# Attention tiles of a decoder step driven by one task, a group of three tiles' parts pinned on TensorE

## The chip, the core and the metric

The kernel runs on one core of a Trainium2 chip. The time is that of the device for one execution, in microseconds (us). Of the core's engines TensorE (PE) multiplies matrices, VectorE (DVE), ScalarE (ACT) and GpSimd (POOL) do elementwise work, reductions and copies, and SyncE (SP) issues most of the transfers.

## What is computed

One step of a two-layer decoder over 1024 prompt tokens and 64 sample tokens (8 sequences of 8), width 1024. Layer 0 mixes by retention (6 heads of 128), layer 1 by dilated sliding-window attention (three groups of four heads of 64), and both also by attention of four heads into 256 memory tokens. Each layer ends with an output projection, a layer norm and a gated feed-forward part. The change touches the two attentions over prompt tokens:

```python
def memory_attention(q, mem_kv):
    sc = jnp.einsum('bshd,bnhd->bhsn', q, mem_kv[:, :, 0]) * MEM_HEAD_DIM ** -0.5
    p = jax.nn.softmax(sc, axis=-1)
    return jnp.einsum('bhsn,bnhd->bshd', p, mem_kv[:, :, 1])

def dilated_prompt(q, k, v, window, dil):
    ...
    sc = jnp.where(valid[:, None], einsum(qb, kk) * d ** -0.5, -jnp.inf)   # this block's keys and the previous block's
    lse = jax.nn.logsumexp(sc, axis=-1)
    p = jnp.exp(sc - lse[..., None])
    o = jnp.einsum('brchqk,brckhd->brcqhd', p, vv)
```

The groups have window and dilation (128, 1), (512, 4) and (2048, 16); their outputs are merged by their softmax denominators.

## The kernel before

All is in fp32. A projection (`dense`) is emulated by three products of split operands (lines L316 to L318, `pd` is the bank they add into). Tokens lie in nine tiles of 128 (eight of prompt, one half tile of samples) and three chunks of 512, 256 and 320 columns.

An attention tile covers 128 tokens and two heads of 64. It has three parts on TensorE, with other engines between them. First the scores, one matmul for each head, which use 64 rows of the array (`S`, L462 in memory attention, L1279 in layer B); the two heads' operands lie in partitions 0 to 63 and 64 to 127. VectorE takes the maximum and ScalarE the exponential (for memory attention VectorE also divides by the sum: L466 to L472; for layer B L1282 to L1287). Then TensorE transposes the probabilities (`mpt` L477, `bpt` L1292) and VectorE copies them (L479, L1294). Last come the output matmuls, which fill 64 columns of the array (`mo` L485, `bo` L1300), and ScalarE copies the result (L149). The trace counts one such fp32 matmul as two instructions, and a transpose as one.

What sets the order: attention tiles are generators which `yield` after each part. The scheduler `S` (class `Streams`) holds them in a queue. A dense step calls `S.tick()` now and then, which lets the first `window` of the queue's active tasks advance in turn; a yielded number is the number of ticks until the task may go on. So the order in which instructions are written mixes dense steps and the parts of several tiles. The tile framework then orders the instructions of each engine once more, by when it expects their operands to be ready, so that a task's instruction can move in front of or behind dense matmuls. Banks of PSUM are shared: four of the pool `pa` serve scores, transposes and outputs.

`mem_prompt(l, T, ...)` is one task for each token tile and covers two pairs of heads in turn (j = 0, 1); main adds eight of them for layer 0 and `layer_b` eight for layer 1. In layer B, `UNITS` lists six units (gi, j): group gi (0 is the local one with dilation 1), pair of heads j. `unit` adds eight `attend` tasks for gi = 1 and 2. For gi = 0 `local_chunk` drives the tiles of one chunk, two at a time, with a `yield` after each part. `row_scores` and `sample` are the samples' attention, `caches` writes cache rows, and `v_tiles` transposes values (`vtr`).

Of the kernel before, what the change touches and what calls it, by code (L numbers as in the profile page):

```python
# [87 lines left out]
def trunk(ctx: ExitStack, tc: tile.TileContext, A: dict, O: dict, g128, g8):  # L88
# [13 lines left out]
    mm = nc.tensor.matmul  # L102
# [10 lines left out]
    SR = (2, 1)  # L113
    SY = (2, 3)
# [254 lines left out]
    def mem_front(sts):  # L369
        mh = [slot([P, 4, 256], F32R, "mh") for _ in range(2)]  # L370
        ml = [slot([P, 4, 256], F32R, "ml") for _ in range(2)]
        for t in range(2):
            for half in range(2):
                b = bank("mtr")
                for i in range(4):
                    nc.tensor.transpose(b[:, i * P:(i + 1) * P], sts[t][:, (half * 4 + i) * P:(half * 4 + i + 1) * P], ident)
# [5 lines left out]
    def mem_kv(l, mh, ml, kt, dst):  # L382
# [3 lines left out]
        for u in range(4):  # L386
# [6 lines left out]
            for i in range(2):  # L393
                nc.tensor.transpose(acc[i][:, u * P:(u + 1) * P], t[:, i * P:(i + 1) * P], ident)
# [5 lines left out]
    def x_task():  # L400
# [10 lines left out]
        for T in range(9):  # L411
# [3 lines left out]
            for half in range(2):  # L415
                b = bank("xtr")
                for i in range(4):
                    nc.tensor.transpose(b[:, i * P:i * P + n], st[:n, (half * 4 + i) * P:(half * 4 + i + 1) * P], ident[:n, :n])
# [35 lines left out]
    def mem_prompt(l, T, kv, kt):  # L454
        yield from wait(("qm", l, chunk_of(T)))
        ts_ = slice(T * P, (T + 1) * P)
        for j in range(2):
            ssum = small(2, "mss")
            sb = [bank("S"), bank("S")]
            for h in range(2):  # L460
                hs = slice(h * 64, (h + 1) * 64)
                mm(sb[h][:, :256], lhsT=mx[hs, 6 + j, ts_], rhs=kt[hs, j, :], start=True, stop=True)  # L462
            nm = small(2, "mnm")
            Pt = rt([P, 2, 256], "mp")
            for h in range(2):
                nc.vector.tensor_reduce(out=nm[:, h:h + 1], in_=sb[h][:, :256], op=ALU.max, axis=AX.X, negate=True)  # L466
                nc.scalar.activation(Pt[:, h, :], sb[h][:, :256], AF.Exp, bias=nm[:, h:h + 1],
                                     accum_out=ssum[:, h:h + 1])
            rs = small(2, "mrs")
            nc.vector.reciprocal(rs, ssum)  # L470
            for h in range(2):
                nc.vector.tensor_scalar(Pt[:, h, :], Pt[:, h, :], rs[:, h:h + 1], None, op0=ALU.mult)  # L472
            yield 1
            pb = bank("mpt")
            for h in range(2):
                for t in range(2):
                    nc.tensor.transpose(pb[:, (2 * h + t) * P:(2 * h + t + 1) * P], Pt[:, h, t * P:(t + 1) * P], ident)  # L477
            pT = rt([P, 512], "mpT")
            nc.vector.tensor_copy(pT, pb)  # L479
            yield 1  # L480
            ob = bank("mo")
            for t in range(2):
                for h in range(2):
                    v0 = 256 + (2 * j + h) * 64
                    mm(ob[h * 64:(h + 1) * 64, :P], lhsT=kv[:, t, v0:v0 + 64], rhs=pT[:, (2 * h + t) * P:(2 * h + t + 1) * P],  # L485
                       start=(t == 0), stop=(t == 1))
            acopy(mx[:, 6 + j, ts_], ob[:, :P])
            yield 1
        done.add(("memT", l, T))

    def mem_sample(l):
# [24 lines left out]
        for b in range(0, 8, 2):  # L516
            kcs, nxt = nxt, [load(b + 2, 0), load(b + 3, 0)]
            kTs = []
            for kc in kcs:
                kb = bank("mkb")  # L520
                for j in range(2):
                    for t in range(2):
                        nc.tensor.transpose(kb[:, (2 * j + t) * P:(2 * j + t + 1) * P], kc[:, t, j * P:(j + 1) * P], ident)
# [21 lines left out]
        for f in range(2):  # L545
            for t in range(2):
                nc.tensor.transpose(pb[:, (2 * f + t) * P:(2 * f + t + 1) * P], Pt[:, f, t * P:(t + 1) * P], ident)
# [15 lines left out]
        for i in range(4):  # L563
            nc.tensor.transpose(tb[:, i * P:(i + 1) * P], on[:, i * P:(i + 1) * P], ident)
# [311 lines left out]
    def y_tiles(c, tiles, grow, brow):  # L876
# [3 lines left out]
        for half in range(2):  # L880
            yield from wait(("y", c, half))
            hs = slice(half * 512, half * 512 + 512)
            for T, n in tiles:
# [3 lines left out]
                for i in range(4):  # L887
                    nc.tensor.transpose(b[:n, i * P:(i + 1) * P], mx[:, half * 4 + i, T * P:T * P + n], ident)
# [87 lines left out]
    def retention(h, qT, kT, V, dmat, dq):  # L976
# [3 lines left out]
        for c in range(3):  # L980
# [14 lines left out]
            for i in range(ni):  # L995
                nc.tensor.transpose(kb[:, i * P:(i + 1) * P], kT[:, c0 + i * P:c0 + (i + 1) * P], ident)
            if samp:
                nc.tensor.transpose(kb[:64, 256:384], kT[:, NP:NT], ident)
# [78 lines left out]
            for i, r in rows:  # L1077
                nc.tensor.transpose(otb[:, i * P:i * P + r], on[:r, i * P:(i + 1) * P], ident[:r, :r])
# [85 lines left out]
    def layer_b():  # L1164
# [35 lines left out]
        def unit(gi, j):  # L1200
# [4 lines left out]
            if gi > 0:  # L1205
# [38 lines left out]
        def caches(gi, j, Kt, V):  # L1244
# [4 lines left out]
            nc.tensor.transpose(bk[:64, :P], Kt[:, NP:NT], ident)  # L1249
# [4 lines left out]
            for q in range(0, len(tiles), 4):  # L1254
                sub = tiles[q:q + 4]
                b = bank("kto")
                for i, T in enumerate(sub):
                    nc.tensor.transpose(b[:, i * P:(i + 1) * P], Kt[:, T * P:(T + 1) * P], ident)
# [6 lines left out]
        def attend(gi, j, T, Qt, Kt, V, oo, om):  # L1265
# [24 lines left out]
            for h in range(2):  # L1290
                for t in range(nt):
                    nc.tensor.transpose(pb[:, (h * nt + t) * P:(h * nt + t + 1) * P], Pt[:, h, t * P:(t + 1) * P], ident)  # L1292
# [24 lines left out]
        def local_chunk(j, c, Qt, Kt, V):  # L1317
# [358 lines left out]
```

## Time and profile before

| | us |
|---|---|
| median of 3 runs | 2707.31 (2706.66 to 2708.17) |
| the profiled execution | 2703.15 |
| its span in the trace | 2701.3 |
| TensorE busy | 2606.2 (96%) |
| VectorE busy | 1821.3 (67%) |
| ScalarE busy | 1200.6 (44%) |
| GpSimd busy | 933.4 (35%) |

A share is an average over all stages. TensorE's is over 90% in nearly all of the 40 slices of the span, and the mean granted clock of the whole run is 0.99 of full speed. Which instruction TensorE waited for, and where, is read from the table of waits; what an instruction costs in its place is read from the starts in the timeline.

### The profile page before, as it was taken

The page shows a single profiled execution, that of the slowest core. Times are in us where ns is not written, and L with a number is a line of the kernel's source. Part 1 is how long each engine was busy: PE and PEld are TensorE (multiplying, and loading weights), DVE is VectorE, ACT ScalarE, POOL GpSimd, SP SyncE. Part 2 cuts the span into 40 slices and gives each one's busy share as a digit, 9 for nine tenths or more (in the row PEclk, how much of TensorE's full clock was granted, in tenths as well). Part 3 has the DMA queues.
Part 4 walks back from the last instruction along what each step waited for, and adds up shares of the span by engine and source line. Part 5 has one row for each costly group of instructions (what it writes and reads, how often), then busy time and mean ns, then how long its engine had stood idle before and what let it go on. Part 6 is the DMA issues. An engine that isn't in the chain of part 4 may idle for free. (4 is left out here: it accounts for less than half of the span.)

```text
span 2701.3 us, 48271 instructions
## 1 busy us (share of the span) xinstructions
PE 2606.2 (96%) x18057; PEld 2360.9 (87%) x18057; DVE 1821.3 (67%) x3843; ACT 1200.6 (44%) x2617; POOL 933.4 (35%) x1118
## 2 busy tenths in 40 slices
PE   8999999999999999999999999989999999999997
PEld 8778888798999989999977777768989998899997
DVE  4534345578777798666684775777987768866666
ACT  4432223344544554444455555544454445344434
POOL 0012223654444443333530111136444444433335
PEclk9999999999999999999999999999999999999998
DMA  7131111134333333332322553552324433433332
GB/s 252 32 95 51 54 48 56 58 93 132 113 113 112 125 100 106 121 103 89 116 91 87 159 163 91 157 148 87 102 91 133 125 119 121 133 114 114 98 96 84
DMA packets 417818, 289.22 MB, mean 107 GB/s; under 512 B 21360, under 2 KB 403120, under 8 KB 415920
## 3 DMA queue, kind: packets, MB, share of 16 engines
q1 hardware_dynamic: 417584, 286.13, 34.4%
q8 instruction: 143, 2.34, 0.4%
q14 instruction: 91, 0.75, 0.1%
HBM read 272.25 MB, written 40.83 MB: 116 GB/s over the span
## 5 line engine op out<-in xcount | busy, mean ns | idle before, releaser
L152 POOL TENSOR_TENSOR wl<-rawu,wh 128x256 fp32r<-128x256 f32 (+1 forms) x560 | 449.7, 827 | 834.1 <-ACT wh L149 748.6
L149 ACT ACTIVATE wh<-raw 128x512 fp32r<-128x512 f32 (+1 forms) x628 | 388.8, 623 | 569.7 <-DVE raw L152 200.2
L316 PE MATMUL pd<-xh,wl 128*128 128x512 f32 (+2 forms) x1200 | 419.4, 350 | 0.8 <-DVE t L439 0.7
L152 DVE TENSOR_TENSOR wl<-raw,wh 128x512 fp32r<-128x512 f32 x460 | 341.8, 747 | 115.3 <-ACT wh L149 111.4
L317 PE MATMUL pd<-xl,wh 128*128 128x512 f32 (+2 forms) x1200 | 407.7, 340 | 0.2 <-DVE xl L152 0.2
L318 PE MATMUL pd<-xh,wh 128*128 128x512 f32 (+2 forms) x1200 | 406.9, 340 | 0.0
L764 PE MATMUL gb<-xh,wl 128*128 128x256 f32 (+1 forms) x1232 | 357.4, 290 | 7.1 <-DVE up L152 3.3
L766 PE MATMUL gb<-xh,wh 128*128 128x256 f32 (+1 forms) x1232 | 356.4, 289 | 0.0
L765 PE MATMUL gb<-xl,wh 128*128 128x256 f32 (+1 forms) x1232 | 353.8, 287 | 0.0
L152 POOL TENSOR_TENSOR wl<-raw,wh 128x256 fp32r<-128x256 f32 x336 | 270.5, 830 | 120.9 <-ACT wh L149 105.5
L764 PE MATMUL pd<-xh,wl 128*128 128x256 f32 (+1 forms) x880 | 255.3, 290 | 7.9 <-DVE up L152 3.9
L149 ACT ACTIVATE wh<-rawu 128x512 fp32r<-128x512 f32 (+1 forms) x280 | 170.9, 614 | 198.9 <-PE pd L816 70.5
L316 PEld LDWEIGHTS pd<-xh,wl 128*128 128x128 f32 x1200 | 227.3, 190 | 36.1 <-issue 16.3
L766 PE MATMUL pd<-xh,wh 128*128 128x256 f32 (+1 forms) x880 | 254.1, 289 | 0.0
L765 PE MATMUL pd<-xl,wh 128*128 128x256 f32 (+1 forms) x880 | 252.1, 286 | 0.0
L317 PEld LDWEIGHTS pd<-xl,wh 128*128 128x128 f32 x1200 | 227.8, 190 | 25.2 <-issue 7.5
L318 PEld LDWEIGHTS pd<-xh,wh 128*128 128x128 f32 x1200 | 227.3, 189 | 24.0 <-issue 5.1
L764 PEld LDWEIGHTS gb<-xh,wl 128*128 128x128 f32 x1232 | 232.7, 189 | 10.0 <-DVE wl L152 3.1
L765 PEld LDWEIGHTS gb<-xl,wh 128*128 128x128 f32 x1232 | 234.4, 190 | 0.6 <-DVE xl L152 0.2
L766 PEld LDWEIGHTS gb<-xh,wh 128*128 128x128 f32 x1232 | 232.4, 189 | 0.0
L814 PE MATMUL gb<-hid,wl 128*128 128x512 f32 (+2 forms) x528 | 174.0, 331 | 4.3 <-ACT hid L149 2.2
L764 PEld LDWEIGHTS pd<-xh,wl 128*128 128x128 f32 x880 | 165.6, 188 | 10.3 <-issue 4.6
(344 smaller groups left out, 6130.5 us busy)
## 6 DMA issues: line engine op xcount, KB each, us to landing
rawu<-in_w_ffn_in_dram SPq DMA_DIRECT2D x88, 512.0 KB
raw<-in_w_ffn_in_dram SPq DMA_DIRECT2D x88, 512.0 KB
raw<-in_w_out_dram SPq DMA_DIRECT2D x32, 512.0 KB
raw<-in_w_ffn_out_dram SPq DMA_DIRECT2D x32, 512.0 KB
rawu<-in_w_ffn_out_dram SPq DMA_DIRECT2D x32, 512.0 KB
out_wins_dram<-in_cache_win_kv_g_dram SPq DMA_DIRECT2D x64, 256.0 KB
qb<-scr_q SPq DMA_DIRECT2D x64, 256.0 KB
raw<-in_w_in_a_dram SPq DMA_DIRECT2D x26, 512.0 KB
```

The source lines that it names most:

```text
L149: nc.scalar.activation(out, in_, AF.Copy, scale=scale)
L152: (eng or nc.vector).tensor_tensor(out=out, in0=a, in1=b, op=op)
L316: mm(out, lhsT=wl, rhs=rh, start=(k == 0), stop=False)
L317: mm(out, lhsT=wh, rhs=rl, start=False, stop=False)
L318: mm(out, lhsT=wh, rhs=rh, start=False, stop=(k == kt - 1))
L764: mm(ps, lhsT=wl[:, k], rhs=XH[:, i, k], start=start and k == 0, stop=False, skip_group_check=True)
L765: mm(ps, lhsT=wh[:, k], rhs=XL[:, i, k], start=False, stop=False, skip_group_check=True)
L766: mm(ps, lhsT=wh[:, k], rhs=XH[:, i, k], start=False, stop=stop and k == 3, skip_group_check=True)
L814: mm(ps, lhsT=wl[:, k], rhs=hid[k][:, 0, ts_], start=first, stop=False)
```

## The change

Matmuls and transposes on TensorE are issued through wrappers that can pin an instruction: it then stays behind the instruction written before it on the same engine, by an edge that only keeps the order. Inside `together()` all of them are pinned, and the first one after it too. A new function `staggered` drives the tiles of one task. Each of its steps starts one more tile and advances all that are under way, the oldest first: the output matmuls of one tile, the transposes of the next and the scores of a third are written one behind the other, inside `together()`. Then it yields a gap: 2 ticks (`MG`, `AG`), and 1 in `local_chunk`. Memory attention becomes one task of 16 pieces (`mem_part`, tile and j), the eight `attend` tiles of a unit one task, and `local_chunk` uses `staggered` in place of two tiles at a time. Ticks, rates and all other constants stay.

```diff
@@ -99,7 +99,27 @@
     pa = pool("pa", 4, space=bass.MemoryType.PSUM)
 
 
-    mm = nc.tensor.matmul
+    pin = {"all": False, "next": False}
+
+    def pinned(ins):
+
+        if pin["all"] or pin["next"]:
+            tc.keep_in_program_order(ins)
+            pin["next"] = pin["all"]
+        return ins
+
+    def mm(*args, **kw):
+        return pinned(nc.tensor.matmul(*args, **kw))
+
+    def transpose(*args):
+        return pinned(nc.tensor.transpose(*args))
+
+    @contextmanager
+    def together():
+        pin["all"] = pin["next"] = True
+        yield
+        pin["all"] = False
+
     dma = nc.sync.dma_start
     S = Streams(3)
     LNY = ((1, 5, 2), (3, 11, 5), (4, 7, 2))
...
@@ -111,6 +131,7 @@
     PA = (6, 4)
     WIN_ = (5, 4)
     SR = (2, 1)
+    MG, AG = 2, 2
     SY = (2, 3)
     RY = (2, 2, 5)
     done = set()
@@ -330,7 +351,7 @@
         b = bank("vtr")
         for i, T in enumerate(tiles):
             a = src(T)
-            nc.tensor.transpose(b[:a.shape[1], i * P:(i + 1) * P], a, ident)
+            transpose(b[:a.shape[1], i * P:(i + 1) * P], a, ident)
         full = [T for T in tiles if T < 8]
         n = len(full)
         if n:
...
@@ -451,42 +472,61 @@
                 S.tick()
             done.add(("qm", l, c))
 
-    def mem_prompt(l, T, kv, kt):
-        yield from wait(("qm", l, chunk_of(T)))
+    def staggered(gens, gap):
+
+
+        live, gens = deque(), deque(gens)
+        while gens or live:
+            if gens:
+                g = gens.popleft()
+                if isinstance(g, tuple):
+                    yield from wait(g[0])
+                    g = g[1]
+                live.append(g)
+            with together():
+                for g in list(live):
+                    if next(g, None) is None:
+                        live.remove(g)
+            yield gap
+
+    def mem_prompt(l, kv, kt):
+
+        yield from staggered([(("qm", l, chunk_of(T)), mem_part(l, T, j, kv, kt)) for T in range(8) for j in range(2)], MG)
+
+    def mem_part(l, T, j, kv, kt):
...
+        yield 1
+        pb = bank("mpt")
...
+        yield 1
+        ob = bank("mo")
...
-            acopy(mx[:, 6 + j, ts_], ob[:, :P])
-            yield 1
-        done.add(("memT", l, T))
+        acopy(mx[:, 6 + j, ts_], ob[:, :P])
+        if j:
+            done.add(("memT", l, T))
...
@@ -1225,9 +1265,8 @@
                 ost = slot([P, 1056], F32, "ost")
                 oo = ost[:, 0:NP].rearrange("p (x r) -> p r x", r=dil)
                 om = ost[:, NP:1056].rearrange("p (t s) -> p t s", t=8)
-                for T in range(8):
-                    r, x0 = (T // 2, T % 2 * P) if gi == 1 else (T, 0)
-                    S.add(attend(gi, j, T, Qt, Kt, V, oo[:, r, x0:x0 + P], om[:, T, :]))
+                place = lambda T: oo[:, T // 2, T % 2 * P:T % 2 * P + P] if gi == 1 else oo[:, T, 0:P]
+                S.add(staggered([attend(gi, j, T, Qt, Kt, V, place(T), om[:, T, :]) for T in range(8)], AG))
                 S.add(spill(gi, j, ost[:, 0:NP], om))
                 S.add(locked(sample(gi, j, Kt, Qt, V)), level=1)
             else:
...
@@ -1328,14 +1367,7 @@
                     dma(rm, scr_m[g - 1][j][ts_].rearrange("(t p) d -> p t d", p=P))
                 res.append(rm)
             gens = [attend(0, j, T, Qt, Kt, V, Qt[:, T * P:(T + 1) * P], res[0][:, i, :]) for i, T in enumerate(tiles)]
-            while gens:
-                for g in gens[:2]:
-                    try:
-                        next(g)
-                    except StopIteration:
-                        gens.remove(g)
-                    yield 0
-                yield 1
+            yield from staggered(gens, 1)
             f = factors([m[:, :, 0:2] for m in res], [m[:, :, 2:4] for m in res], n, 2)
             for g in range(3):
                 fe = rt([P, 512], "fe")
...
@@ -1508,8 +1540,7 @@
             done.add(("msamp", j))
 
         qm_dense(1)
-        for T in range(8):
-            S.add(mem_prompt(1, T, kv, kt))
+        S.add(mem_prompt(1, kv, kt))
         S.add(locked(mem_sample(1)))
         for gi, j in UNITS:
             if gi == 1 and j == 1:
...
@@ -1559,8 +1590,7 @@
     S.until(lambda: ("x", 2) in done)
     S.rate, S.at = RT[1], TK[0]
     qm_dense(0)
-    for T in range(8):
-        S.add(mem_prompt(0, T, kv, kt))
+    S.add(mem_prompt(0, kv, kt))
     S.add(locked(mem_sample(0)))
     layer_a()
     S.rate = RT[2]
```

All other calls of `nc.tensor.transpose` become `transpose`, as in the hunk of `v_tiles`. The instructions of each engine are the same in number.

On TensorE before, in layer 1's memory attention, transposes (`mpt`), outputs of several tiles (`mo`) and scores of three pairs (`S`) stand in a row, each row of the order being one or more instructions of a kind:

```order
L318 MATMUL pd<-xh,wh 128x256
L316 MATMUL pd<-xh,wl 128x256
L477 MATMUL mpt<-kmain,mp 128x128 x4
L485 MATMUL mo<-mpT,mx 64x128 x20
L462 MATMUL S<-mx 128x256 x6
L317 MATMUL pd<-xl,wh 128x256
L318 MATMUL pd<-xh,wh 128x256
```

On TensorE after, at a group of the same attention, the lines are those of the wrappers (L112 matmul, L115 transpose), `mkb` and `mstb` belong to the samples' memory attention:

```order
L115 MATMUL mkb<-kmain,mkc 128x128 x4
L112 MATMUL mo<-mpT,mx 64x128 x4
L115 MATMUL mpt<-kmain,mp 128x128 x4
L112 MATMUL S<-mx 128x256 x2
L112 MATMUL mstb<-mkT,mx 32x256 x4
L112 MATMUL pd<-xh,wl 128x256
```

Outputs of one tile, transposes of the next and one pair of scores now stand together, and runs of 20 and 6 no longer occur there.

On TensorE before, in the local attention of unit (0,1), first chunk, the scores of the third and fourth tile stand apart among dense matmuls:

```order
L1300 MATMUL bo<-bpT,V 64x128 x4
L1279 MATMUL S<-Kt,mx 128x256 x2
L316 MATMUL pd<-xh,wl 128x320
L317 MATMUL pd<-xl,wh 128x320
L318 MATMUL pd<-xh,wh 128x320
L316 MATMUL pd<-xh,wl 128x320
L317 MATMUL pd<-xl,wh 128x320
L318 MATMUL pd<-xh,wh 128x320
L316 MATMUL pd<-xh,wl 128x320
L317 MATMUL pd<-xl,wh 128x320
L318 MATMUL pd<-xh,wh 128x320
L1279 MATMUL S<-Kt,mx 128x256 x2
```

On TensorE after, the same tiles of the same unit, with three value transposes (`vtr`) between:

```order
L112 MATMUL bo<-bpT,V 64x128 x2
L115 MATMUL bpt<-kmain,bp 128x128 x4
L112 MATMUL S<-Kt,mx 128x256 x2
L115 MATMUL vtr<-kmain,vT 128x128 x2
L115 MATMUL vtr<-kmain,vT 64x128
L112 MATMUL bo<-bpT,V 64x128 x4
L115 MATMUL bpt<-kmain,bp 128x128 x4
L112 MATMUL S<-Kt,mx 128x256 x2
L112 MATMUL pd<-xh,wl 128x320
```

Nine dense matmuls between the two pairs of scores have moved away; between a pair's scores and its transposes stand three `vtr` and one tile's outputs.

## Rows read from the trace of the kernel before

**Rows 1.** Table by stretches, the two that the change reorders (stretch; length, busy, instructions, clock)

```profile
74.30:210.40 136.10, 130.49 (x889) 102.79 (x888) 63.65 (x177) 53.66 (x145) 15.98 (x17) 1.00 0.21 63
1387.80:1855.30 467.50, 444.96 (x3014) 337.57 (x3013) 308.35 (x927) 244.75 (x696) 86.71 (x98) 0.99 0.43 125
```

**Rows 2.** Waits of TensorE, 74.3 to 210.4 us (total us, times, longest)

```profile
PE S L462 <- ACT mp L467: 2.8, 4, 0.7
PE mpt L477 <- DVE mp L472: 1.6, 2, 1.2
PE mo L485 <- DVE mpT L479: 0.7, 1, 0.7
```

**Rows 3.** Waits of TensorE, 1387.8 to 1855.3 us, those of attention

```profile
PE bo L1300 <- DVE bpT L1294: 3.3, 3, 1.6
...
PE S L462 <- ACT mp L467: 1.8, 3, 0.7
...
PE bpt L1292 <- ACT bp L1287: 1.4, 2, 1.2
...
PE S L1279 <- DVE ost L1282: 0.9, 1, 0.9
```

**Rows 4.** Timeline of TensorE, 1398 us (start, duration, line, out<-in, array, tile)

```profile
1398.43 0.70 PE L462 MATMUL S<-mx 64*128 64x256 f32 x4
1399.07 0.50 PE L316 MATMUL pd<-xh,wl 128*128 128x512 f32 x1
1399.40 0.40 PE L317 MATMUL pd<-xl,wh 128*128 128x512 f32 x1
...
1399.87 0.40 PE L316 MATMUL pd<-xh,wl 128*128 128x512 f32 x1
1400.20 0.70 PE L462 MATMUL S<-mx 64*128 64x256 f32 x2
1400.82 0.50 PE L317 MATMUL pd<-xl,wh 128*128 128x512 f32 x1
```

**Rows 5.** Timeline of TensorE, three tiles' scores in a row

```profile
73.80 1.13 PE L462 MATMUL S<-mx 64*128 64x256 f32 x8
75.60 1.15 PE L462 MATMUL S<-mx 64*128 64x256 f32 x4 [0.67 <-ACT mp L467]
76.69 0.50 PE L316 MATMUL pd<-xh,wl 128*128 128x512 f32 x1
```

**Rows 6.** Timeline of TensorE, transposes beside transposes and between scores

```profile
1546.95 0.27 PE L1473 MATMUL spt<-kmain,spp 128*128 128x128 f32 x1
1547.06 0.27 PE L1474 MATMUL spt<-kmain,spp 128*64 128x128 f32 x1
...
1562.62 0.44 PE L1292 MATMUL bpt<-kmain,bp 128*128 128x128 f32 x2
1562.98 0.70 PE L1279 MATMUL S<-Kt,mx 64*128 64x256 f32 x2
```

**Rows 7.** Timeline of TensorE, the output matmuls of a tile

```profile
1460.48 0.66 PE L485 MATMUL mo<-mpT,mx 128*64 128x128 f32 x8
1461.07 0.41 PE L317 MATMUL pd<-xl,wh 128*128 128x320 f32 x1
```

**Rows 8.** Timeline of VectorE, softmax of a memory tile

```profile
127.17 0.75 DVE L466 TENSOR_REDUCE mnm<-S 128x1 f32<-128x256 f32 x2 [2.41 <-PE S L462]
...
128.88 0.62 DVE L472 TENSOR_SCALAR mp<-mp,mrs 128x256 f32<-128x256 f32 x2
```

**Rows 9.** Timelines of TensorE and ScalarE, a layer-B tile's scores and last exponential

```profile
1544.28 0.70 PE L1279 MATMUL S<-Kt,mx 64*128 64x256 f32 x4
...
1546.53 0.49 ACT L1287 ACTIVATE bp<-bp,bnm 128x256 f32<-128x256 f32 x1
```

**Rows 10.** Timelines of TensorE and VectorE, a late pair's scores and their first reader

```profile
1769.14 0.70 PE L1279 MATMUL S<-Kt,mx 64*128 64x256 f32 x4
...
1776.87 0.41 DVE L1282 CUSTOM_DVE_ANT_0 bp<-S,masks 128x256 f32<-128x256 f32 x1
```

More of the change, by code (lines that the diff above doesn't have):

```diff
@@ L1 @@
 from collections import deque
-from contextlib import ExitStack
+from contextlib import ExitStack, contextmanager
 import concourse.bass as bass
@@ L375, in mem_front @@
                 for i in range(4):
-                    nc.tensor.transpose(b[:, i * P:(i + 1) * P], sts[t][:, (half * 4 + i) * P:(half * 4 + i + 1) * P], ident)
+                    transpose(b[:, i * P:(i + 1) * P], sts[t][:, (half * 4 + i) * P:(half * 4 + i + 1) * P], ident)
                 bv = b.rearrange("p (k t) -> p k t", k=4)
@@ L417, in x_task @@
                 for i in range(4):
-                    nc.tensor.transpose(b[:, i * P:i * P + n], st[:n, (half * 4 + i) * P:(half * 4 + i + 1) * P], ident[:n, :n])
+                    transpose(b[:, i * P:i * P + n], st[:n, (half * 4 + i) * P:(half * 4 + i + 1) * P], ident[:n, :n])
                 bv = b.rearrange("p (k t) -> p k t", k=4)[:, :, :n]
@@ new lines, in mem_part @@
+    def mem_part(l, T, j, kv, kt):
+        ts_ = slice(T * P, (T + 1) * P)
+        ssum = small(2, "mss")
+        sb = [bank("S"), bank("S")]
+        for h in range(2):
+            hs = slice(h * 64, (h + 1) * 64)
+            mm(sb[h][:, :256], lhsT=mx[hs, 6 + j, ts_], rhs=kt[hs, j, :], start=True, stop=True)
+        nm = small(2, "mnm")
+        Pt = rt([P, 2, 256], "mp")
+        for h in range(2):
+            nc.vector.tensor_reduce(out=nm[:, h:h + 1], in_=sb[h][:, :256], op=ALU.max, axis=AX.X, negate=True)
+            nc.scalar.activation(Pt[:, h, :], sb[h][:, :256], AF.Exp, bias=nm[:, h:h + 1],
+                                 accum_out=ssum[:, h:h + 1])
+        rs = small(2, "mrs")
+        nc.vector.reciprocal(rs, ssum)
+        for h in range(2):
+            nc.vector.tensor_scalar(Pt[:, h, :], Pt[:, h, :], rs[:, h:h + 1], None, op0=ALU.mult)
+        yield 1
+        pb = bank("mpt")
+        for h in range(2):
+            for t in range(2):
+                transpose(pb[:, (2 * h + t) * P:(2 * h + t + 1) * P], Pt[:, h, t * P:(t + 1) * P], ident)
+        pT = rt([P, 512], "mpT")
+        nc.vector.tensor_copy(pT, pb)
+        yield 1
+        ob = bank("mo")
+        for t in range(2):
+            for h in range(2):
+                v0 = 256 + (2 * j + h) * 64
+                mm(ob[h * 64:(h + 1) * 64, :P], lhsT=kv[:, t, v0:v0 + 64], rhs=pT[:, (2 * h + t) * P:(2 * h + t + 1) * P],
+                   start=(t == 0), stop=(t == 1))
+        acopy(mx[:, 6 + j, ts_], ob[:, :P])
+        if j:
+            done.add(("memT", l, T))
@@ L887, in y_tiles @@
                 for i in range(4):
-                    nc.tensor.transpose(b[:n, i * P:(i + 1) * P], mx[:, half * 4 + i, T * P:T * P + n], ident)
+                    transpose(b[:n, i * P:(i + 1) * P], mx[:, half * 4 + i, T * P:T * P + n], ident)
                 nc.vector.bn_stats(out=st6[T][:n, half * 6:half * 6 + 6], in_=b[:n])
@@ L1248, in caches @@
             bk = bank("kns")
-            nc.tensor.transpose(bk[:64, :P], Kt[:, NP:NT], ident)
+            transpose(bk[:64, :P], Kt[:, NP:NT], ident)
             acopy(kn, bk[:64, :P])
@@ L1444, in sample @@
                 mm(sb[:, P:192], lhsT=qc, rhs=Kt[:, NP:NT], start=True, stop=True)
-                nc.tensor.transpose(sb[:, 0:P], sT, ident)
+                transpose(sb[:, 0:P], sT, ident)
             else:
@@ L1454, in sample @@
                 for i in range(4):
-                    nc.tensor.transpose(kb[:, i * P:(i + 1) * P], kc[:, i, :], ident)
+                    transpose(kb[:, i * P:(i + 1) * P], kc[:, i, :], ident)
                 kT = rt([P, 512], "kT")
@@ L1524, in ln_params @@
         b = bank("lnt")
-        nc.tensor.transpose(b[:, :64], st, ident[:64, :64])
+        transpose(b[:, :64], st, ident[:64, :64])
         nc.vector.tensor_copy(lnp, b[:, :64])
```

57 lines of the change are left out of this document (14 added, 43 removed).

## The prediction

> **What bounds the kernel now.** I began with the page's busy shares: TensorE is busy for 96% of the span and the next engine, VectorE, for 67%, so the end moves only by what TensorE's own stream gains or loses. I then laid the two programs' orders side by side. They differ in two stretches alone, which in the trace of before are 74.3 to 210.4 us and 1387.8 to 1855.3 us, and every engine executes the same number of instructions in both programs. The table by stretches [rows 1] gives what can be had there at all: 136.10 − 130.49 = 5.6 us of TensorE idle in the first, 467.50 − 444.96 = 22.5 us in the second. The table of waits [rows 2, 3] says how much of this idle belongs to the instructions that the change moves. Then I read the timeline of TensorE for the price of an instruction in its place, by start to start, since the durations of pipelined matmuls overlap.
>
> **What goes.** The waits of the attention parts are 2.8 + 1.6 + 0.7 = 5.1 us in the first stretch [rows 2] and 3.3 + 1.8 + 1.4 + 0.9 = 7.4 us in the second [rows 3]. The largest, scores waiting for the exponent of the tile before, has a visible cause: three tiles' scores stand in a row and find no free bank for the third. Such a run takes 76.69 − 73.80 = 2.89 us [rows 5] where three pairs at 0.64 us (a pair is 1398.43 to 1399.07) [rows 4] need 1.92. There are six such runs, so 6 × 1.0 = 6.0 us, of which the waits show 2.8 + 1.8 = 4.6; 1.4 us come on top. After the change a group holds one pair only, and 5.1 + 7.4 + 1.4 = **13.9 us go**.
>
> **What the new grouping costs in TensorE's own time.** A run of scores or output matmuls works on half the array (64 rows or 64 columns), and changing over costs time. Two dense matmuls go from 1399.40 to 1399.87, 0.235 us each. The one ahead of a score run takes 1399.87 to 1400.20, 0.33, and the one behind such a run 1399.07 to 1399.40, 0.33 [rows 4]: 0.093 us on the way in and 0.10 on the way out. A transpose takes 0.11 us (1546.95 to 1547.06), but two of them between two score runs 0.36 (1562.62 to 1562.98) [rows 6]: 0.22, the 0.093 of the way in to the next run, and 0.05 on the way out to a transpose. I counted the runs in both orders over the two stretches. Of scores there are 60 before and 87 after, of output matmuls 63 and 81, of other small ones 93 and 90. Entries from full-array work rise by 40 (+40 × 0.093 = +3.7 us), exits to dense matmuls fall by 12 (−12 × 0.10 = −1.2), and exits to transposes rise by 48 (+48 × 0.055 = +2.7). Against this, one head alone (1400.20 to 1400.82) costs 0.62, as much as the pair [rows 4]: the two heads of a pair lie on different halves of the array and run beside each other. Before, 18 heads stand alone; after, 14, six of them with 256 columns and eight with 128. With this and with output matmuls in shorter runs (a tile's four take 0.59 us, 1460.48 to 1461.07 [rows 7]), the runs' own time falls by 2.5 us by my count. So **+2.7 us**: the pinning joins three parts of three tiles, but it doesn't make TensorE's stream shorter. Had the count of alternating runs been priced at nothing, the term would be −2.5; had every change of run cost the highest of these prices, 0.10, it would be about +5.
>
> In the Trainium skill, "TensorE: Matmul & The Clock Gate" (Part 2, step 1, and Part 3, on what overlaps) has TensorE pull a weight load ahead of running matmuls when the row groups don't conflict or the load goes to the background buffer. By that the way out of a score run into a transpose could be hidden, and the term would be near −2.5 us; the 0.33 us in the place of 0.235 speaks against it for these shapes [rows 4].
>
> **What is late next.** In the new order each group's transposes need the softmax of the previous group's scores, and its output matmuls the copy of the transposes. For memory attention the softmax ends with the two scalings, 2.4 us after the scores: the reduction begins at 127.17, the last scaling ends at 128.88 + 0.62 = 129.50 [rows 8]. For a layer-B tile with 256 keys it is 2.1 us: scores end at 1544.28 + 0.63 = 1544.91, the last exponential at 1546.53 + 0.49 = 1547.02 [rows 9]. I added up the work that the new order puts on TensorE between a group's scores and the next one's transposes. In layer 0 it is 5 to 8 us and nothing waits. In layer 1's memory attention it is 2.4 to 7 us, once short by 0.1. In units (1,0) and (1,1) it is mostly 2.5 to 5 us but once 1.52, short by 0.6. In the local attention's first chunk the tiles follow at a gap of 1, and the stretches are 2.06, 1.36 and 1.00 us: short by 0.7 and 1.1. The last is the one shown in the order, three value transposes (3 × 0.11 + 0.05) and a tile's output matmuls (0.59 + 0.093). This comes twice, once for each j, so 2 × (0.6 + 0.7 + 1.1) = 4.8 us; two later local tiles have 1.92 and 1.40, short by 0.2 and 0.7. Together 4.8 + 0.9 + 0.1 = **5.8 us come**. Behind a pinned instruction that waits the whole of TensorE waits, dense matmuls included, so none of this hides. It would be nothing if the softmax were quicker, and it is more wherever VectorE or ScalarE has something queued in front.
>
> VectorE, ScalarE and GpSimd do what they did, and the weight DMAs are issued by the same dense steps, so I cost these at nothing. What hides them is that VectorE is busy for 308 of 467 us and ScalarE for 245 in the long stretch [rows 1]; without that cover the price is the slower rival's.
>
> **Sum.** −13.9 + 2.7 + 5.8 = −5.4 us against the profiled execution's own 2703.15 us, so 2697.8. That execution is 4.2 us under the median of the runs shown, 2707.31, and the changed kernel is timed as those were: 2707.3 − 5.4 = **2702 us**. Its own range comes from the terms: −13.9 could be −10 if a third of the removed waits only move, the grouping −2.5 to +5, the new waits 3 to 9; some −10 to 0 us, most of it within 2697 to 2706.
>
> **Rivals.** *Larger gain.* 22.5 − 7.4 = 15.1 us of TensorE's idle in the long stretch belongs to work outside the attention tiles [rows 1, 3]. If the one-tile-at-a-time pace spreads the load of VectorE and ScalarE, half of it could go too: −5.4 − 7.5 = −13, 2694 us. For it speaks that the waits are short and on VectorE or ScalarE; against it, that nothing leaves these engines.
>
> *No change.* Coming earlier to the same operands, TensorE waits longer there. If a third of what goes, 4.6 us, turns up at those other waits, −0.8 remains: 2706.5 us. For it: the idle outside attention is larger than inside. Against it: much of the removed wait lies in layer 0 and in the memory part [rows 2], where there is little other idle.
>
> *Slower, by VectorE's backlog.* Late in layer B VectorE carries the sample scores too. There the scores of one pair end at 1769.14 + 0.63 = 1769.77, and VectorE takes them up at 1776.87 only [rows 10], 7.1 us later; with the op and the exponentials, about 2.1 us as in [rows 9], the transposes are possible after 9.2 us. Before, TensorE has 4 to 9 us of other work for such pairs, placed by readiness. After, the pinned order leaves 1.4 to 4.3 us at three pairs. If the backlog meets them as it met this pair, each waits 9.2 − 2.9 = 6.3 us: +19, and −5.4 + 19 = +13.6, 2721 us. From 1.8 us of backlog at each of the three it eats the whole gain. For it: that row. Against it: a waiting TensorE lets VectorE catch up, and VectorE's own order moves with the change, so that the pair need not meet the backlog.
>
> *It doesn't do what it says.* The pins could be without effect if readiness had put the same instructions there anyway; the orders speak against it, since each group stands unbroken after and no such group stands before. Its time would be that of before, and I give it no chance of its own.
>
> **How the numbers follow.** Forecast 0.42, larger gain 0.15, no change 0.20, slower 0.23. About 0.2% (5.4 us) is what a measurement of this kernel can tell from no change. The forecast lies on that bound, so I give 0.24 of its 0.42 to faster and 0.18 to no change; with the larger gain faster is 0.39. No change has 0.18 + 0.20 + 0.01 of a mild backlog = 0.39; slower 0.22. The range for eight in ten runs from 2690, a little under the larger gain, to 2717, which leaves out the worse half of the slower case; the forecast's own is 2697 to 2706.
>
> **What would show it.** Right: the score waits of [rows 2, 3] gone, first stretch shorter by 2 to 5 us, new waits of transposes for the exponential of 0.5 to 1.1 us in the local attention, TensorE's busy time in the two stretches up by 1 to 4 us. Wrong: TensorE's busy time lower by several us (changes of run are cheaper, or lone heads dearer, than I priced); transposes waiting 3 us or more at once (the backlog); or the waits of value transposes, row scores and sample matmuls longer by what attention has lost.

## The result, and the profile after

The changed kernel takes 2719.04 us (median of 4 runs, 2717.26 to 2724.65), the kernel before 2706.98 us (2703.51 to 2708.17): ratio 1.005, interval 1.0032 to 1.0068. It is slower by 12.06 us (2719.04 − 2706.98), where 5.4 us less was forecast; the time lies outside the range. The two profiled executions stand further apart, at spans of 2701.3 and 2718.3 us, because that of before, at 2703.15 us, is 3.8 us under its median and that of the changed kernel, at 2720.20, 1.2 above. One median below holds a run far off the others: one of the 12 runs of `loose` took 3571 us, and without it its median would be 2701.5 in place of 2702.1.

The same matmul can be found in both traces, since each stretch holds the same instructions, so the table by stretches can be taken between matching places. First column the stretch, then its length, the busy time of TensorE, of its weight loads, VectorE, ScalarE and GpSimd, the granted clock, the DMA share and GB/s. After:

```profile
75.22:204.49 129.27, 129.04 (x888) 99.90 (x886) 65.09 (x178) 57.10 (x148) 15.52 (x17) 1.00 0.22 66
1383.19:1874.71 491.52, 456.93 (x3012) 338.26 (x3013) 310.62 (x929) 244.97 (x695) 85.53 (x97) 0.97 0.41 118
```

And before, at the same instructions (the stretches of [rows 1], from the first to the last instruction that moved):

```profile
74.33:210.36 136.03, 130.41 (x889) 102.74 (x885) 63.65 (x177) 53.66 (x145) 15.96 (x17) 1.00 0.21 63
1387.82:1855.29 467.47, 444.93 (x3013) 337.55 (x3013) 308.32 (x927) 244.73 (x696) 86.70 (x98) 0.99 0.43 125
```

The first stretch, layer 0's memory attention, is 136.03 − 129.27 = 6.76 us shorter: TensorE's idle falls from 5.62 to 0.23 us, its busy time by 1.37. The second, layer B, is 24.05 us longer: idle 22.54 to 34.59 (+12.05), busy +12.0. So in these two executions one half of the change works and the other costs more than three times that gain. Small differences outside (together −0.3 us) make up the span's +17.0.

The waits of TensorE in the second stretch after (total us, times, longest), to set against [rows 3]:

```profile
PE bpt L115 <- ACT bp L1326: 10.6, 11, 2.4
PE sob L112 <- DMA vc<-in_cache_win_kv_g_dram: 7.6, 5, 3.0
PE bo L112 <- DVE bpT L1333: 2.2, 3, 1.1
PE sqt L115 <- DVE sT L1426: 2.1, 1, 2.1
PE smt L115 <- DVE smo L1531: 1.8, 2, 1.0
PE spt L115 <- ACT spp L1502: 1.8, 1, 1.8
```

Before, of the rows that [rows 3] does not show:

```profile
PE sob L1485 <- DMA vc<-in_cache_win_kv_g_dram: 1.1, 2, 0.9
```

The waits of scores are gone, as forecast. Transposes waiting for the exponential have grown from 1.4 to 10.6 us, and the samples' value matmuls (`sob`), which wait for a transfer of cached values, from 1.1 to 7.6. How one of the latter sits in TensorE's timeline:

```profile
1554.63 0.43 PE L112 MATMUL sob<-vc,zz 128*32 128x128 f32 x8 [3.04 <-DMA vc<-in_cache_win_kv_g_dram]
1554.99 0.66 PE L112 MATMUL bo<-bpT,V 128*64 128x128 f32 x8
1555.58 0.69 PE L115 MATMUL bpt<-kmain,bp 128*128 128x128 f32 x2
```

A group of attention (`bo`, `bpt`) follows right behind a matmul that waits 3 us, and nothing passes.

The rest of the longer stretch is busy time. The table by 10 us, after, in the local attention of unit (0,1):

```profile
1775.00:1785.00 10.00, 7.16 (x55) 5.98 (x53) 7.13 (x21) 3.83 (x11) 3.36 (x4) 1.00 0.85 160
1785.00:1795.00 10.00, 7.95 (x38) 4.42 (x38) 8.20 (x24) 5.32 (x19) 1.41 (x2) 0.63 0.33 98
1795.00:1805.00 10.00, 9.49 (x62) 7.67 (x62) 8.84 (x29) 6.24 (x18) 3.56 (x4) 0.85 0.18 47
```

TensorE is idle for 2.8 us of one stretch, and in the next the granted clock is 0.63, so part of it is at 1.2 GHz. What that does to the instructions is seen in the timeline, below the scores of the chunk's first tile and their first reader on VectorE:

```profile
1780.48 0.49 PE L112 MATMUL S<-Kt,mx 64*128 64x128 f32 x4
1784.14 0.28 DVE L1321 CUSTOM_DVE_ANT_0 bp<-S,masks 128x128 f32<-128x128 f32 x1
...
1785.68 0.71 PE L115 MATMUL bpt<-kmain,bp 128*128 128x128 f32 x2 [2.45 <-ACT bp L1326]
...
1789.41 1.18 PE L115 MATMUL bpt<-kmain,bp 128*128 128x128 f32 x4 [0.45 <-ACT bp L1326]
1790.52 1.23 PE L112 MATMUL S<-Kt,mx 64*128 64x256 f32 x4
1791.67 0.90 PE L115 MATMUL vtr<-kmain,vT 128*128 128x128 f32 x3
```

A pair of scores takes 1791.67 − 1790.52 = 1.15 us where it takes 0.64 at 2.4 GHz [rows 4]. Summing (1 − clock) × 10 us over layer B gives 5.1 us before and 13.7 after: up to 8.6 of the 12.0 us of added busy time, and at least 3.4 for the changed order. The 8.6 is an upper bound, since a low clock costs nothing while TensorE idles, and it is that of these two executions: in the first experiment, where layer B is as before, the sum is 8.6 in place of 5.1.

### The profile page after: what moved, and what is told of

Its sections match the earlier page's. It is cut to its first block, busy times and chain, and to the rows that moved or that the text cites. A ratio compares the mean times of both kernels' runs of the same rounds, so it can differ in the third digit from the quotient of the medians.

```text
span 2718.3 us, 48315 instructions
## 1 busy us (share of the span) xinstructions
PE 2614.2 (96%) x18057; PEld 2355.3 (87%) x18057; DVE 1824.0 (67%) x3843; ACT 1204.4 (44%) x2621; POOL 931.5 (34%) x1118
## 5 line engine op out<-in xcount | busy, mean ns | idle before, releaser
L112 PE MATMUL pd<-xh,wl 128*128 128x256 f32 (+3 forms) x2080 | 678.9, 327 | 9.0 <-DVE up L173 3.9
L112 PE MATMUL pd<-xh,wh 128*128 128x256 f32 (+3 forms) x2080 | 658.7, 317 | 0.0
L112 PE MATMUL pd<-xl,wh 128*128 128x256 f32 (+3 forms) x2080 | 657.1, 316 | 0.2 <-DVE xl L173 0.2
L112 PEld LDWEIGHTS pd<-xh,wl 128*128 128x128 f32 x2080 | 393.8, 190 | 53.3 <-issue 25.3
L112 PEld LDWEIGHTS pd<-xh,wh 128*128 128x128 f32 x2080 | 393.6, 189 | 23.1 <-issue 2.5
L112 PEld LDWEIGHTS pd<-xl,wh 128*128 128x128 f32 x2080 | 395.8, 190 | 19.5 <-DVE xl L173 1.1
L112 PE MATMUL gb<-xh,wl 128*128 128x256 f32 (+1 forms) x1232 | 357.2, 290 | 7.2 <-DVE up L173 3.3
L112 PE MATMUL gb<-xh,wh 128*128 128x256 f32 (+1 forms) x1232 | 356.3, 289 | 0.0
L112 PE MATMUL gb<-xl,wh 128*128 128x256 f32 (+1 forms) x1232 | 353.6, 287 | 0.0
L112 PE MATMUL gb<-hid,wh 128*128 128x320 f32 (+2 forms) x1056 | 251.6, 329 | 0.0
L112 PE MATMUL pd<-hid,wh 128*128 128x256 f32 (+2 forms) x1018 | 241.5, 328 | 0.4 <-DVE hid L173 0.4
L112 PEld LDWEIGHTS gb<-xh,wl 128*128 128x128 f32 x1232 | 232.5, 189 | 10.1 <-DVE wl L173 3.2
L112 PEld LDWEIGHTS gb<-xl,wh 128*128 128x128 f32 x1232 | 234.0, 190 | 0.6 <-DVE xl L173 0.2
L112 PEld LDWEIGHTS gb<-xh,wh 128*128 128x128 f32 x1232 | 232.2, 188 | 0.0
L112 PEld LDWEIGHTS gb<-hid,wh 128*128 128x128 f32 x1056 | 180.1, 189 | 14.2 <-DVE hid L173 0.6
L112 PEld LDWEIGHTS pd<-hid,wh 128*128 128x128 f32 x1018 | 173.4, 190 | 14.7 <-DVE hid L173 0.9
L112 PE MATMUL gb<-hid,wl 128*128 128x512 f32 (+2 forms) x528 | 173.9, 331 | 4.3 <-ACT hid L170 2.2
```

The lines of the kernel that those rows point to most:

```text
L112: return pinned(nc.tensor.matmul(*args, **kw))
```

## Experiments

They ran in four sets, each on one chip together with the kernel before, whose median was 2708.5 to 2709.0 us. The changed kernel was not run again: it is taken as 12.06 us above the kernel before of each set, with an interval of 8.7 to 18.4 from its own four runs, so that differences from it of a few us are weak. Layer B of an unchanged program varies too: in the first experiment it took 470.47 us where the profile of before has 467.47, so a difference of 3 us in one trace says little.

**Which half.** Layer 0 alone (`mem0`), and layer 1 alone (`layerb`):

```diff
# mem0: layer 1's memory attention, the units' tiles and the local attention are written as before
-        S.add(mem_prompt(1, kv, kt))
+        for T in range(8):
+            S.add(mem_prompt_old(1, T, kv, kt))
# layerb: the same for layer 0 only
-    S.add(mem_prompt(0, kv, kt))
+    for T in range(8):
+        S.add(mem_prompt_old(0, T, kv, kt))
```

> Only layer 0's memory attention is one staggered, pinned task; layer 1 is as before. Theory (layer 0 gains, layer B loses): the first stretch is shorter by 6.8 us as in the changed kernel's trace (136.0 to 129.3), nothing else moves: 6 to 7 us below before, about 2700. Rival (the gain in layer 0 is only handed to a later wait): within 2 us of before.

> The reverse: layer 0 as before, layer 1's memory attention, units and local attention staggered and pinned. Theory: the second stretch is 24 us longer in the profiles (467.5 to 491.5), so some 19 to 24 us above before, 2726 to 2731. Rival (the profiles compared differ by 4 us between executions of one kernel, and part of the 24 is that): 2720 to 2726.

`mem0`: 2702.99 us, ratio 0.998 (0.997 to 0.999), 5.96 below before. `layerb`: 2727.28 us, 1.0073 (1.0061 to 1.0085), 18.3 above. Layer 0 gains and layer B loses, as both theories had it, but the loss is 18.3 us in the medians where the profiles show 24.05: the 5.7 between them belong to the two executions profiled, as its rival supposed, though the time itself is in the theory's range. The five runs of `layerb` have a mean granted clock of 0.989, as the 27 of before in this set have, so how much of the loss in the medians is clock is not shown. The first stretch of `mem0`, columns as above:

```profile
74.76:204.49 129.73, 129.01 (x888) 99.88 (x887) 65.11 (x178) 57.05 (x148) 15.51 (x17) 1.00 0.22 66
```

The second stretch of `layerb`:

```profile
1392.25:1884.14 491.89, 456.51 (x3012) 338.35 (x3013) 310.63 (x929) 245.51 (x695) 85.08 (x97) 0.98 0.43 118
```

They repeat the changed kernel's 129.27 and 491.52, and the medians of the two halves add up to its loss (−5.96 + 18.33 = 12.4).

**The local attention and the pins.**

```diff
# nolocal: local_chunk as before, two tiles at a time
-            yield from staggered(gens, 1)
+            while gens:
+                for g in gens[:2]:
...
# nopin: no pins at all
-        pin["all"] = pin["next"] = True
+        pin["all"] = pin["next"] = False
```

> The changed kernel with the local attention driven two tiles at a time as before. Theory (the tiles of the local attention follow too closely, at a gap of 1, and TensorE waits for the exponential): the waits of transposes for the exponential fall from 10.6 to 3 us or less, the clock dips behind them go too, 10 to 14 us below the changed kernel, 2705 to 2709. Rival (the loss is in the units' tiles and in the samples' value loads, 7.6 us of waits): no more than 5 us below it, 2714 to 2719.

> The changed kernel staggered but with no pins: readiness orders the parts. Theory (a pinned instruction that waits holds dense matmuls that are ready): the waits for the exponential fall under 4 us and the time to about 2707 to 2711. Rival (the staggering, that is how many ticks lie between a tile's parts, sets the loss; the pins only keep it visible): within 4 us of the changed kernel, 2715 to 2723.

`nolocal`: 2708.53 us, 1.0005 (0.9993 to 1.0017), 12.5 below the changed kernel; waits for the exponential 1.6 us. Its theory holds. `nopin`: 2714.78 us, 1.0023 (1.0014 to 1.0032), 6 below it, at neither expectation. Its two stretches show why:

```profile
75.01:204.69 129.68, 129.25 (x888) 99.97 (x886) 65.32 (x178) 57.04 (x148) 15.53 (x17) 1.00 0.22 66
1382.01:1864.90 482.89, 466.75 (x3013) 342.94 (x3013) 310.00 (x931) 244.86 (x698) 83.82 (x97) 0.99 0.43 121
```

The first is as short as in the changed kernel, so layer 0's gain is the staggering's and needs no pins. In the second idle is down to 16.1 us, less than before, but TensorE is busy for 466.75, 22 us more than before: without pins the order of the staggered tiles tears the two heads of a score pair apart (70 runs of one head alone in layer B's order, 14 in the changed kernel). So the pins do two things, a good one and a bad one.

**Distance, softmax, VectorE's load, and the pins at a group's ends.**

```diff
# lgap3
-            yield from staggered(gens, 1)
+            yield from staggered(gens, 3)
# dec: in the local attention
-                    transpose(..., Pt[:, h, t * P:(t + 1) * P], ident)
+                    transpose(..., Kt[:, (2 * h + t) * P:(2 * h + t + 1) * P], ident)
# thin: row scores of one element, copied in place of their sum
-                tt(qb, qb, bc(kc, 2, [P, 2, 2, P]), ALU.mult)
+                tt(qb[:, :, :, 0:1], qb[:, :, :, 0:1], ..., ALU.mult)
# loose: only inside a group
-        if pin["all"] or pin["next"]:
-            tc.keep_in_program_order(ins)
-            pin["next"] = pin["all"]
+        if pin["all"]:
+            if pin["next"]:
+                tc.keep_in_program_order(ins)
+            pin["next"] = True
...
-        pin["all"] = pin["next"] = True
+        pin["all"], pin["next"] = True, False
```

> The changed kernel with a gap of 3 ticks in place of 1 between the local attention's groups. Theory (the loss in local attention is the distance alone): waits of transposes for the exponential fall from 10.6 to under 2 us and the time to that of the kernel with the old local attention, 2706 to 2711. Rival (pinned groups of the local attention lose at any distance, by what stands in front of them): above 2714.

> The changed kernel, but the local attention's transposes read columns of the keys in place of the probabilities, so they never wait for the softmax, which is still computed (its result is left out). Theory: the waits for the exponential that belong to local attention go (10.6 to about 2 us), and with them the clock dips of these stretches (TensorE busy in layer B from 456.9 towards 449): 10 to 17 us below the changed kernel, 2702 to 2709. Rival (the clock dips come from the many small matmuls, not from the waits): the waits go but TensorE's busy time stays within 2 us of 456.9, 2709 to 2713.

> The changed kernel with the samples' row scores cut to one element of each row (multiplication and reduction of 64 or 128 elements left out), which takes most of VectorE's work beside the local attention away. Rival theory of the prediction (VectorE's backlog makes the local tiles late): the waits for the exponential fall from 10.6 to 5 us or less, 6 to 10 us below the changed kernel, 2709 to 2713. Theory of the short distance: only the first tile's wait of 2.4 us goes, the others of 0.4 to 1.5 stay, 2 to 4 us below, 2715 to 2717.

> The changed kernel with pins only inside a group: its first instruction isn't held behind what was written before it, nor what follows behind the group. Theory (the outer pins put the samples' value matmuls, which wait for a transfer, in front of groups that are ready): the waits of these matmuls fall from 7.6 to under 2 us, as with no pins at all, and the time by 4 to 8 us, 2711 to 2715. Rival (the transfers are late in themselves): these waits stay above 5 us, 2717 to 2721.

`lgap3`: 2723.28 us, 1.0058 (1.0042 to 1.0073). No faster than the changed kernel, against the theory and with the rival: the waits for the exponential fall to 2.0 us, but others grow, transfers of cached values 8.0, the samples' `stb` 5.4, `bo` 3.4. `dec`: 2712.54, 1.0011 (1.0002 to 1.0021), 8.5 below the changed kernel (12.06 − 3.6): the waits for the exponential fall to 1.9 us, but `bo` waits 5.7 and `sob` 8.6. Its layer B:

```profile
1382.76:1869.06 486.30, 451.87 (x3012) 337.03 (x3013) 313.49 (x929) 244.42 (x695) 83.34 (x97) 0.98 0.42 120
```

Idle is 486.30 − 451.87 = 34.4 us, as in the changed kernel (34.6), though 8.7 us of waits for the exponential are gone; TensorE's busy time is 5 us less, with a clock sum of 8.5. The time is in the rival's range, the busy time as the theory had it.

`thin`: 2713.29, 1.0017 (1.0008 to 1.0026). VectorE's busy time falls from 310.6 to 251.5 us in the stretch, and the waits for the exponential still stand at 9.0 of 10.6. So its backlog is not what makes most of them. Yet the time is 7.7 us below the changed kernel; the wait of `sob` falls from 7.6 to 3.6, the clock sum from 13.7 to 10.2. Whether the same lighter VectorE would speed up the kernel before as well was not run, so VectorE's part in the loss of time stays open.

`loose`: 2702.1, 0.9975 (0.9965 to 0.9985), some 19 us below the changed kernel (12.06 + 6.84), far more than expected. Its layer B:

```profile
1382.84:1854.29 471.45, 448.72 (x3014) 334.11 (x3013) 310.87 (x931) 245.52 (x698) 83.81 (x97) 0.99 0.44 124
```

And its waits there:

```profile
PE bpt L116 <- ACT bp L1327: 5.8, 9, 1.4
PE bo L113 <- DVE bpT L1334: 3.9, 6, 1.7
...
PE sob L113 <- DMA vc<-in_cache_win_kv_g_dram: 1.0, 1, 1.0
```

Idle 22.7 us as before, busy 448.7, the clock's sum 5.1 again. The tiles, ticks and gaps are those of the changed kernel. What the inner pins are good for shows in the rows of scores by form, here without any pin (count, busy us, mean ns):

```profile
L112 PE MATMUL S<-Kt,mx 64*128 64x256 f32 x88 | 27.9, 428 | 0.0
L112 PE MATMUL S<-Kt,mx 64*128 64x128 f32 x104 | 21.4, 323 | 0.0
```

And with inner pins:

```profile
L113 PE MATMUL S<-Kt,mx 64*128 64x256 f32 x88 | 16.8, 428 | 0.0
L113 PE MATMUL S<-Kt,mx 64*128 64x128 f32 x104 | 15.2, 323 | 0.0
```

The same 192 instructions of the same mean length keep TensorE busy for 49.3 or for 32.0 us: kept in pairs, the two heads run beside each other.

**Which outer pin, and is distance a loss of its own?**

```diff
# headpin: no pin on what follows a group
-        if pin["all"] or pin["next"]:
+        if pin["all"]:
             tc.keep_in_program_order(ins)
-            pin["next"] = pin["all"]
# tailpin: no pin on a group's first instruction
-        if pin["all"] or pin["next"]:
+        if pin["next"]:
             tc.keep_in_program_order(ins)
-            pin["next"] = pin["all"]
+        pin["next"] = pin["all"]
...
-        pin["all"] = pin["next"] = True
+        pin["all"], pin["next"] = True, False
# loose_old = loose + nolocal; loose_lgap3 = loose + lgap3
```

> The changed kernel without the pin on the instruction behind a group; the group's first instruction stays pinned behind what was written before it. Theory (the pin in front keeps the samples' value matmuls, which wait for a transfer, ahead of the group): waits for that transfer 5 us or more, 2714 to 2719. Rival (the pin behind the group is the costly one: it keeps later work, dense matmuls too, from passing a group that waits): the time falls to 2702 to 2707.

> The reverse: a group's first instruction is free, the instruction behind the group stays pinned. Theory (the pin in front is the costly one): 2702 to 2708, waits for the value transfer under 2 us. Rival (the pin behind): 2713 to 2719. If both of these two kernels stay above 2713, either pin alone is enough to tie groups and sample matmuls into one chain.

> Pins only inside a group, and the local attention two tiles at a time as before. Theory (outer pins and the local attention's distance are separate losses, 17 and 10 us of the changed kernel): the waits for the exponential fall from 5.8 to 2 us or less and 5 to 10 us go, 2692 to 2697. Rival (the two are one loss, a waiting group that nothing may pass, and free groups have cured it): within 3 us of the kernel with inner pins, 2699 to 2705.

> Pins only inside a group, and a gap of 3 ticks in the local attention. It stood at 2723 with the outer pins, where the waits moved from the exponential to the samples' work pinned in front of groups. Theory (those are the outer pins' waits): 2695 to 2703, the waits of samples' work under 4 us. Rival (at a gap of 3 the local attention is late for the output projection whatever the pins): above 2710.

`headpin`: 2708.18, 0.9995 (0.9985 to 1.0005), the wait of `sob` is 0.5 us. `tailpin`: 2714.97, 1.0022 (1.0013 to 1.0031), the waits for the exponential 13.6 us in 18 times. Layer B of `headpin`, then of `tailpin`:

```profile
1384.80:1861.75 476.95, 453.43 (x3013) 336.72 (x3013) 311.76 (x929) 245.81 (x695) 84.89 (x97) 0.98 0.44 122
1384.34:1870.29 485.95, 452.72 (x3014) 334.62 (x3013) 313.75 (x931) 244.94 (x698) 84.98 (x97) 0.99 0.43 120
```

The theory of the front pin falls, and the rival holds, 1 us past its range in `headpin`: over `loose` the pin in front costs 6 us, the one behind 13, both 19. The pin behind brings the idle: 33.2 us with it alone, against 23.5 with the front pin alone, 22.7 in `loose` and 34.6 with both. `sob` waits long for its transfer only with both, and in `tailpin` the idle is there without that wait. The clock doesn't follow the idle: its sum is 10.3 us in `headpin` and 5.1 in `tailpin`. `loose_old`: 2702.84, 0.9975 (0.9965 to 0.9985), the same as `loose`: with free ends the local attention's distance costs nothing that can be measured, so it was not a loss of its own, as the rival had it. (In its trace idle is 18.0 us against 22.7, and the clock sum 10.3 against 5.1.) `loose_lgap3`: 2709.92, 1.0005 (0.9995 to 1.0015): 13 below `lgap3`, by the outer pins, and yet 8 above `loose`, between both expectations and next to the rival's. In its layer B idle is 22.1 us, as in `loose`; busy time is 7.8 more, with a clock sum of 11.9 against 5.1.

**Is the transfer a cause?**

```diff
# vcfree; vcfree_dec = vcfree + dec
-                    mm(ob[rows], lhsT=wp, rhs=vc[:, i, :], ...)
+                    mm(ob[rows], lhsT=wp, rhs=V[:, i, :], ...)
```

> The changed kernel, but the samples' value matmuls read the unit's own values in place of the cached values, which are still loaded (the samples' result is wrong by that), so that they never wait for a transfer. Theory (behind both outer pins a wait of these matmuls stops everything): their 7.6 us go, 5 to 9 us below the changed kernel, 2710 to 2714. Rival (TensorE would wait for the next softmax instead): waits for the exponential rise by 4 us or more and the time stays within 3 us, 2716 to 2720.

> Both cuts at once: samples' value matmuls without the transfer, and local attention's transposes without the softmax. Theory (these two waits and the clock behind them are the whole loss of layer B): about 2700, 2697 to 2705. Rival (a third wait takes their place, as the copies behind the transposes did when only the softmax was cut): 2706 or more.

`vcfree`: 2726.27, 1.0064 (1.0052 to 1.0076): not faster than the changed kernel at all, and outside both expectations. Its waits in layer B:

```profile
PE bpt L115 <- ACT bp L1326: 13.4, 13, 2.1
PE smt L115 <- DVE smo L1531: 3.6, 2, 2.2
PE bo L112 <- DVE bpT L1333: 2.8, 3, 1.8
PE sqt L115 <- DVE sT L1426: 2.2, 1, 2.2
```

The transfer's 7.6 us are gone from the list, and the other rows have grown by 2.8, 1.8, 0.6 and 0.1. Layer B's length is 491.13 us, unchanged. `vcfree_dec`: 2716.38, 1.0031 (1.0018 to 1.0043), the rival's side: with both waits taken away, `bo` waits 5.3, the units' transposes 6.9. The edit does more than take a wait away, though: free of the transfer, some 116 of the 300 `sob` instructions stand at another place in TensorE's order, some between a group's transposes. So these two runs do not settle by themselves whether the transfer is a cause. `dec`, where only 68 of TensorE's 18057 instructions stand elsewhere, and `tailpin`, which has the idle without this wait, say the same with less doubt: a row of the table of waits is where TensorE stood, not why.

## Why the prediction was wrong

**What bounds the kernel**, and where the difference lies: right. Only the two stretches changed.

**What goes** (−13.9): right in layer 0, where 5.39 us of idle went against 5.1 forecast, and `mem0` gained 5.96 us. In layer B the score waits of [rows 3] went, the waits of `bo` fell only from 3.3 to 2.2, and the new waits were larger than all that went.

**The grouping's own cost** (+2.7): near, as far as the clock can be taken off. Busy time changed by −1.4 in the first stretch and by at least +3.4 in the second, 12.0 less the clock's 8.6 at most. `loose` has the same groups and the clock sum of before: −1.2 in the first stretch (129.19 − 130.41), +3.8 in the second, +2.6 together. But `tailpin`, at the same clock sum, has +7.8 in the second, so the ends matter here too. The prediction's −2.5 for a hidden way out was worked out wrongly: with the exits to transposes free the term is 2.7 − 2.7, about 0, and −2.5 needs every change of run to be free. The Trainium skill ("TensorE: Matmul & The Clock Gate", Part 2, step 1) has a weight load pulled ahead of running matmuls when the row groups don't conflict or the load goes to the background buffer; `loose` fits the price of [rows 4, 6] better than either 0 or −2.5. But I looked at the runs only as a cost; I didn't see that staggering without pins would tear pairs apart, and that pins could keep them whole and that this would be worth 17 us of score time (49.3 − 32.0) against staggering without them.

**What is late next** (+5.8): this is the step that failed. I added up the work between a group's scores and its transposes, and set it against a softmax's time. By that, transposes were to wait 5.7 us for the exponential in the units and the local attention; they waited 10.6. The local attention has 9.7 of it in place of 4.5, a unit (2,1) that I hadn't named 0.9 (at 1686.86), and units (1,0) and (1,1), which I had priced at 1.2, none. One of these waits, 2.45 us at 1785.68, had VectorE's other work in front of it: the scores of that tile start at 1780.48 and VectorE takes them up at 1784.14. The next two in that chunk were 0.45 and 0.86 us, near what I had worked out.

What I left out is what the pins tie together at a group's two ends. I wrote that behind a waiting pinned instruction all of TensorE waits, and then counted the waits of attention alone. But a group's first instruction is tied to whatever was written before it, and the one written behind it to the group; these are often the samples' matmuls and transposes, which wait for their own operands (`sob` 7.6 us after, 1.1 before), and I priced their waits at nothing. Idle in layer B rose by 12.05 us where the terms −7.4 and +5.8 let me expect a fall of about 2. Freed ends bring it back to 22.7 us and give 19 us of time (`loose`), and the pin behind the group alone puts 10.5 us of idle on again (`tailpin`). Taking one wait away does not: the idle stays at 34.4 us in `dec` and 35.5 in `lgap3`. That each end passes its neighbour's wait on is my reading of these runs; no run follows a single wait along the chain.

**At nothing** I costed TensorE's clock, by leaving it out. In the two profiled executions it was up to 8.6 us. It is no fixed price of the idle: the sum is 13.7 us in the changed kernel and 5.1 in `loose`, but 5.1 in `tailpin` with 33.2 us of idle and 10.3 in `loose_old` with 18.0. What it adds to the medians is not shown.

**The rivals.** The time of 2719.04 is close to that of the slower rival, 2721 us, but by luck: its three waits of 6.3 us for VectorE's backlog do not occur, the longest being 2.45 us, and with most of VectorE's row scores gone the waits for the exponential stay at 9.0 of 10.6 us (`thin`). The backlog of [rows 10] met one tile, that of 2.45 us. The 7.7 us that `thin` gains by other ways stay unexplained. That the change does not do what it says is out: `nopin` and `loose` show how much the pins hold.

**What stays open.** The experiments that leave outer pins in move waits from row to row, so the 12 us of idle cannot be divided among the instructions that show them. The pin behind the group brings the idle; the front pin's 6 us stand in busy time (453.4 against 448.7 us in `loose`) beside a clock sum 5.2 us higher, so how much of them is the pin's own is not shown. The same holds for the 8 us of `loose_lgap3` over `loose`.

The kernel with inner pins only, 2702.1 us, beats both: 6.8 us under before and some 19 under the changed kernel. Most of the 6.8 is layer 0's, since `mem0` alone has 5.96; in layer B grouping with free ends is worth no more than the spread.

## What to carry to other kernels

Where staggering tears apart what must run side by side (two heads on two halves of the array), pin that, and try the ends of the group free: here the two order edges to neighbours cost 19 us, the one behind the group more than the one in front. When a pinned stream waits, the row of the table of waits names the place only; take the wait away before calling it a cause, and look whether the order stayed the same. Layer 0, where the work between dependent parts is two to three times their latency (5 to 8 us against 2.4), took pinned ends without a wait; the local attention, with 1 to 2 us, did not, and with free ends it was no loss.

## What the runs showed of the hardware

A pair of scores on two row halves took 0.64 us and one head alone 0.62 [rows 4]; torn apart over a layer this was 49.3 against 32.0 us. In the changed kernel a few microseconds of waiting were followed by stretches at a granted clock of 0.63 and 0.85, in which a pair took 1.15 us. Over layer B this was 8.6 us at most, beside 12.05 of added idle. Waiting alone did not decide it: `tailpin`, with as much idle, had a clock sum of 5.1 us, that of the kernel before.
